# A transformer step's feed-forward input matrix: seven products of quarter sums in place of eight of quarters

## The chip, the cores and the metric

The kernel runs on one core of a Trainium2 chip. The metric is the time of one execution on the device, in microseconds (us); lower is better. A core has five engines that run side by side and wait for each other by semaphores: TensorE (PE, matmuls into the PSUM memory), VectorE (DVE), ScalarE (ACT), GpSimd (POOL) and SyncE (SP, which issues the DMAs here). Each works through its own instructions strictly in the order in which they were issued.

## The reference

One step of a one-layer hybrid encoder on 544 tokens (512 of a prompt, 32 of a sample), model width 1024: a norm, a combined input projection, three branches (differential attention, a gated linear recurrence, cross-attention), gates, an output projection; then the feed-forward block, which is what the change is about:

```
h2 = rms_norm(x, norm_ffn)
g_ff, u_ff = split(h2 @ w_ffn_in, 2)      # w_ffn_in: 1024 x 5632, so two halves of 2816
x = x + (silu(g_ff) * u_ff) @ w_ffn_out   # w_ffn_out: 2816 x 1024
y = rms_norm(x, norm_final)
```

All is float32. The kernel multiplies at that precision with three matmuls in a fast rounded format: each operand is split into a rounded part ("hi", made by ACT, line 236) and the remainder ("lo", made by DVE with `LO`, line 249), and hi x hi, hi x lo and lo x hi are added up in PSUM.

## The kernel before, in words

Activations lie transposed: 128 channels in the partitions, 8 blocks of channels (k) by 544 tokens (T) along the free side. The weights come in chunks of 1024 x 256 (1 MB each), two tiles of 128 output channels per chunk. `load_weights` fetches chunk after chunk into two raw buffers, `split_weights` splits each tile (128 x 1024) into hi (ACT) and lo (DVE); three buffers of each stand between it and PE. `gemm` runs a tile: 8 k x 2 halves of the tokens (272 columns each) x 3 = 48 matmuls into an accumulator of two PSUM banks (two accumulators, "acc"), and then spawns the tile's evacuation.

The feed-forward block has 22 chunks of w_ffn_in, 11 for the gate and 11 for the up half, in three parts (`FF_PARTS`). `ff_gate` multiplies the accumulator by the norm factor `rb` and applies Silu, `ff_up` multiplies by `rb` and by the gate and splits the result for the second matrix. The plain form does not need `rb` for its matmuls: the input (`xgh`, `xgl`) is x times the norm's gain, and `rb` comes in when the result is taken out of PSUM. `rb` itself comes from `row_norm`, spawned by `out_evac` after the last tile of the output projection (w_out). The order of stages is in for part 0, in 1, out 0, in 2, out 1, out 2. The last three tiles of the last out stage run in two halves of tokens, so that the final norm of the first half lies under the second.

The order of the instructions on each engine is made when the program is built. `Flow` is a planner in which every step is a generator; it counts an assumed cost for each instruction (about 1 ns per element for DVE, 0.9 for ACT, 0.4 per column for PE), and resumes a step when the buffers and results that it asked for are due by that count. What it issues first on an engine runs first there, whatever the real times are.

Of the kernel before, what the change touches and what calls it, by code (L numbers as in the profile page):

```python
# [9 lines left out]
F32 = mybir.dt.float32  # L10
F32R = mybir.dt.float32r
# [36 lines left out]
class Flow:  # L48
# [6 lines left out]
    def __init__(self):  # L55
        self.now = 0.0
        self.free = {"A": 0.0, "V": 0.0, "G": 0.0, "D": 0.0, "port": 0.0}
        self.rdy = {}
        self.heap = []
        self.blocked = []  # L60
        self.seq = 0
        self.ev = {}
        self.slots = {}

    @staticmethod
    def span(ap):
# [100 lines left out]

    def give(self, tag, at=None):
        self.slots[tag].append(self.now if at is None else at)

    def set(self, ev, at=None):
        self.ev[ev] = self.now if at is None else at
# [17 lines left out]
def hybrid_step(ctx: ExitStack, tc, io):  # L190
# [113 lines left out]
            fl.ready(out, t + 2200)  # L304
        return t + 2200

    def MM(out, lhsT, rhs, start, stop):
        nc.tensor.matmul(out, lhsT=lhsT, rhs=rhs, start=start, stop=stop)  # L308
# [42 lines left out]
    c_fi, c_fo = [None] * 3, [None] * 3  # L351
    for kind, i in (("in", 0), ("in", 1), ("out", 0), ("in", 2), ("out", 1), ("out", 2)):
# [10 lines left out]
    def load_weights():  # L363
        for i, (src, nk) in enumerate(chunks):
# [13 lines left out]
            for j in range(2):  # L378
                if ("raw", i, j) not in fl.ev:
                    fl.set(("raw", i, j), t)  # L380

    def split_weights():
        for i, (src, nk) in enumerate(chunks):
            if i in c_mem[4:]:
# [12 lines left out]
                fl.give("raw", t2)  # L397
                continue
            for j in range(2):
                yield from fl.get(("raw", i, j))  # L400
                yield from fl.take("wh", "wl")
                wh = slot_tile(wpool, [P, 8, P], F32R, "wh")[:, :nk]
                wl = slot_tile(wpool, [P, 8, P], F32R, "wl")[:, :nk]
                r = raws[i][:, :nk, j * P:(j + 1) * P]
                t = VC(wh, r) if fl.free["V"] + 1500 < fl.free["A"] else A(wh, r)
                wts[i, j] = (wh, wl)
# [4 lines left out]
            fl.give("raw", t2)  # L411

    def gemm(tiles, xh, xl, n=T, need=None):

# [3 lines left out]
        def products(acc, c, j, seq, first, last):  # L418
            wh, wl = wts[c, j]
            for q, (a, b, k) in enumerate(seq):  # L420
                w, x = (wl if a else wh), (xl if b else xh)
                for hf, m in halves:
                    s = slice(hf * m, (hf + 1) * m)
                    MM(acc[:, hf, :m], w[:, k, :], x[k][:, s] if isinstance(x, list) else x[:, k, s],
                       start=first and q == 0, stop=last and q == len(seq) - 1)
                yield None

        def finish(acc, c, j, evac):
            fl.give("wh")
            fl.give("wl")  # L430
            fl.spawn(evac(acc), fl.now + 60)

        if need is None:
# [1090 lines left out]
        return go  # L1524


    acts = [None] * 3

    def ff_gate(i, n):
        def go(acc):  # L1530
# [25 lines left out]
            fl.set(("f", i, n), t)  # L1556
        return go

    def ffn_in(i):
        f0, nf = FF_PARTS[i]  # L1560
        pool, a, b = (actp, "ah", "al") if i % 2 == 0 else (S["actb"], "bh", "bl")
        acts[i] = (tl(pool, [P, KD, T], F32R, a), tl(pool, [P, KD, T], F32R, b))
        for c in range(nf // 2):
            need = (lambda k: ("xg", k)) if i == 0 and c == 0 else None
            yield from gemm([(c_fi[i][c][0], j, ff_gate(i, 2 * c + j)) for j in range(2)], xgh, xgl, need=need)
            yield from gemm([(c_fi[i][c][1], j, ff_up(i, 2 * c + j)) for j in range(2)], xgh, xgl)

    def fo_evac(fp, i, n):
        def go(acc):
            t = VT(b2(x2[:, n]), acc[:, :, :HT], b2(x2[:, n]), OP.add)  # L1570
            give_acc(t)
            if i < 2:
                return
            yield t
            yield from square_sum(S["sq"][0], n)
        return go
# [42 lines left out]
    def ffn_out(fp, i):  # L1619
        f0, nf = FF_PARTS[i]  # L1620
        fh, flo = acts[i]
        split = 0 if i < 2 else LAST
# [7 lines left out]
        for t0, m_ in ((0, 256), (256, T - 256)):  # L1630
            for c, j, n in tiles[KD - split:]:
# [3 lines left out]
                for q, (a, k) in enumerate([(a, k) for a in range(2) for k in range(nf)]):  # L1635
                    if a == 1 and k == 0:
                        yield from fl.get(("wl", c, j))
                    for x in (fh, flo) if a == 0 else (fh,):
                        MM(acc, wts[c, j][a][:, k], x[:, k, t0:t0 + m_], q == 0 and x is fh,
                           q == 2 * nf - 1)  # L1640
                    yield None
                fl.spawn(last_evac(fp, n, (t0, m_), acc), fl.now + 60)
# [5 lines left out]
    def main():  # L1648
# [77 lines left out]
        xgh = tl(hpool, [P, KD, T], F32R, "hh")  # L1726
        xgl = tl(hpool, [P, KD, T], F32R, "hl")
# [3 lines left out]
        yield from ffn_in(0)  # L1731
        yield from ffn_in(1)
# [12 lines left out]
def host_arrays(inputs):  # L1745
# [71 lines left out]
```

## Time and profile before

| | |
|---|---|
| three runs, us | 1231.04, 1229.99, 1230.53; median 1230.53 |
| profiled execution, us | 1230.78, its span 1229.0 |
| busy in the span | PE 1214.2 us (99%), DVE 678.9 (55%), ACT 466.0 (38%), POOL 28.2 (2%) |
| DMA | 131.19 MB, mean 107 GB/s |
| mean granted clock of TensorE | 0.993 |

Busy time of an engine is the time in which one of its instructions ran; the span goes from the first to the last instruction. A matmul's shown duration overlaps with its neighbours', so its price is read from start to start. The granted clock is the share of TensorE's full 2.4 GHz; it has two levels, 0.5 and 1.

### The profile page before, as it was taken

The numbers are of one execution on the slowest core, as the hardware profiler recorded it, in microseconds if no ns is written. First come the engines' busy times: TensorE is split into PE (matmuls) and PEld (weight loads), VectorE is DVE, ScalarE is ACT, GpSimd is POOL, SyncE is SP. The second block draws the span as 40 slices with busy tenths as digits, with TensorE's granted clock in tenths as the row PEclk, the third lists the DMA queues.
The fourth block names the chain that finished last, engine by engine and source line by source line (L and its number), as shares of the span: only waits on it lengthen the run. The fifth ranks groups of instructions, "written<-read, shape, count | busy, mean of one in ns | idle before, by whom it ended". The sixth has DMA issues, their size and how long they took to land.

```text
span 1229.0 us, 22475 instructions
## 1 busy us (share of the span) xinstructions
PE 1214.2 (99%) x9620; PEld 1205.5 (98%) x9620; DVE 678.9 (55%) x1340; ACT 466.0 (38%) x781; POOL 28.2 (2%) x88
## 2 busy tenths in 40 slices
PE   8999999999999999999999999999999999999996
PEld 8999999999999999999999999999999999999996
DVE  6886878787257777654455244544443443344335
ACT  6635454444335665532333232332222221222122
POOL 0002000000001001000000000000000000000001
PEclk8999999999999999999999999999999999999998
DMA  7772343321222223323422413131323222222212
GB/s 261 233 272 96 133 138 116 106 87 54 103 97 94 78 73 109 122 69 121 140 95 76 176 69 104 69 104 69 103 70 103 72 101 90 82 96 77 87 52 73
DMA packets 36835, 131.19 MB, mean 107 GB/s; under 512 B 4184, under 2 KB 15832, under 8 KB 25088
## 3 DMA queue, kind: packets, MB, share of 16 engines
q1 hardware_dynamic: 36736, 129.76, 30.9%
q8 instruction: 75, 1.23, 0.4%
q14 instruction: 24, 0.20, 0.0%
HBM read 118.81 MB, written 13.68 MB: 108 GB/s over the span
## 4 chain that ended last, share of the span: by engine, by line
PE 96%; DVE 2%; DMA 1%; ACT 0%; issue 0%; SPq 0%; DVEq 0%; ACTq 0%
PE acc L308 86%; PE side L308 8%; PE side L315 2%; DMA mk_d<-mkf 1%; DMA raw<-in_w_mem_kv 0%; DVE x L258 0%; DVE wl L249 0%; DVE xT L258 0%; DVE rst L249 0%; DVE al L249 0%; ACT wh L236 0%; DVE m L249 0%; ACT m L236 0%; SPq L300 0%; DVE hl L249 0%
## 5 line engine op out<-in xcount | busy, mean ns | idle before, releaser
L308 PE MATMUL acc<-hh,wh 128*128 128x272 f32 x1856 | 387.1, 289 | 0.0
L308 PE MATMUL acc<-hl,wh 128*128 128x272 f32 x1856 | 385.8, 289 | 0.0
L236 ACT ACTIVATE wh<-raw 128x1024 fp32r<-128x1024 f32 (+1 forms) x179 | 187.4, 1048 | 351.2 <-PE acc L308 328.3
L308 PEld LDWEIGHTS acc<-hh,wh 128*128 128x128 f32 x1856 | 290.7, 189 | 0.3
L308 PEld LDWEIGHTS acc<-hl,wh 128*128 128x128 f32 x1856 | 290.0, 188 | 0.1
L249 DVE TENSOR_TENSOR wl<-raw,wh 128x1024 fp32r<-128x1024 f32 (+1 forms) x180 | 217.1, 1207 | 95.6 <-PE acc L308 73.6
L308 PE MATMUL acc<-hh,wl 128*128 128x272 f32 x1856 | 257.2, 288 | 0.0
L308 PEld LDWEIGHTS acc<-hh,wl 128*128 128x128 f32 x1856 | 241.5, 188 | 0.1
L249 DVE TENSOR_TENSOR t<-acc,rb 128x544 f32<-128x544 f32 x44 | 31.9, 725 | 150.3 <-PE acc L308 150.0
L308 PE MATMUL acc<-ah,wh 128*128 128x272 f32 (+2 forms) x480 | 101.4, 288 | 0.0
L308 PE MATMUL acc<-al,wh 128*128 128x272 f32 (+2 forms) x480 | 101.4, 289 | 0.0
L249 DVE TENSOR_TENSOR x<-acc,x 128x544 f32<-128x544 f32 (+2 forms) x35 | 23.6, 675 | 102.7 <-PE acc L308 102.7
L308 PE MATMUL acc<-bl,wh 128*128 128x272 f32 x384 | 79.7, 289 | 0.0
L308 PE MATMUL acc<-bh,wh 128*128 128x272 f32 x384 | 79.6, 288 | 0.0
L308 PEld LDWEIGHTS acc<-ah,wh 128*128 128x128 f32 x480 | 76.4, 188 | 0.0
L308 PEld LDWEIGHTS acc<-al,wh 128*128 128x128 f32 x480 | 76.2, 188 | 0.0
L308 PE MATMUL acc<-ah,wl 128*128 128x272 f32 (+2 forms) x480 | 66.0, 288 | 0.0
L308 PEld LDWEIGHTS acc<-ah,wl 128*128 128x128 f32 x480 | 62.4, 188 | 0.0
L308 PEld LDWEIGHTS acc<-bh,wh 128*128 128x128 f32 x384 | 60.1, 189 | 0.0
L308 PEld LDWEIGHTS acc<-bl,wh 128*128 128x128 f32 x384 | 60.0, 188 | 0.0
L308 PE MATMUL acc<-bh,wl 128*128 128x272 f32 x384 | 54.0, 289 | 0.0
L308 PEld LDWEIGHTS acc<-bh,wl 128*128 128x128 f32 x384 | 50.0, 188 | 0.0
(250 smaller groups left out, 1318.1 us busy)
## 6 DMA issues: line engine op xcount, KB each, us to landing
raw<-in_w_in SPq DMA_DIRECT2D x24, 1024.0 KB, 4.9
raw<-in_w_ffn_in SPq DMA_DIRECT2D x22, 1024.0 KB, 4.9
raw<-in_w_gate SPq DMA_DIRECT2D x12, 1024.0 KB, 4.9
raw<-in_w_ffn_out SPq DMA_DIRECT2D x8, 1024.0 KB, 4.9
raw<-in_w_mem_kv SPq DMA_DIRECT2D x7, 1024.0 KB, 6.1
raw<-in_w_proj_a SPq DMA_DIRECT2D x4, 1024.0 KB, 4.9
raw<-in_w_proj_b SPq DMA_DIRECT2D x4, 1024.0 KB, 4.8
raw<-in_w_proj_c SPq DMA_DIRECT2D x4, 1024.0 KB, 4.9
```

The costliest lines, as they stand in the source:

```text
L236: nc.scalar.activation(out, in_, func, scale=scale, bias=bias, accum_out=accum_out)
L249: nc.vector.tensor_tensor(out, a, b, o)
L308: nc.tensor.matmul(out, lhsT=lhsT, rhs=rhs, start=start, stop=stop)
L315: nc.tensor.transpose(out, in_, ident[:n, :n])
```

## The change

Take a chunk's 1024 x 256 weights as 2 x 2 quarters: by output tile (first or second 128 columns) and by k (even or odd blocks of channels). Take the activations as 2 x 2 quarters: by k (even, odd) and by tokens (first, second 272). Eight products of quarters make the four quarters of the result; Winograd's form of Strassen's scheme does it with seven products of sums of quarters. Of the 22 chunks, the first gate chunk and the first up chunk (`FF_PLAIN`) stay as they were; the other 20 (`FF_FAST`) use seven products, each of 4 k-blocks x 3 = 12 matmuls of 272 columns.

- **Weights.** `split_ffn` splits blocks of 128 x 512 (a quarter or a sum of quarters) in place of tiles; the three buffers are cut into six such blocks, and two more come from the space of `ah`/`al` after the plain chunks. The four sums of a chunk are made by DVE, mostly in place in the raw buffer. A22 and P4 of a chunk are split after A11 of the next (`split_late`), and the raw buffer is given back then. The host stores w_ffn_in so that each quarter is contiguous.
- **Activations.** `ff_forms` makes the normalised activations (with `rb` in them) and their sums once, in four groups (B11, B2, U1, U2), each split in hi and lo.
- **Products.** `seven` runs the products of a chunk in the order A11, (A22 and P4 of the chunk before), A12, P2, P1, P3. P2 and P3 go on adding to the accumulator of A11; between them `quarters` copies the state out: events c11 (after A11), c12 (after P2), u3 (after P3) and c22 (the sum with P1's bank).
- **Parts.** Four parts of 6, 6, 6 and 4 tiles in place of three, in the order in 0 and 1, out 0, in 2, out 1, in 3, out 2, out 3; the seven products run in three runs, of 5, 3 and 2 pairs of gate and up chunk.

```diff
-    FF_PARTS = [(0, 8), (8, 8), (16, 6)]
+    FF_PARTS = [(0, 6), (6, 6), (12, 6), (18, 4)]
+    FF_ORDER = [("in", 0), ("in", 1), ("out", 0), ("in", 2), ("out", 1), ("in", 3), ("out", 2), ("out", 3)]
+    FF_PLAIN = c_fi[0][0]
+    FF_FAST = {c for part in c_fi for pair in part for c in pair} - set(FF_PLAIN)
...
+    def split(name, src):
+        yield from fl.take("hb", "lb")
+        n = src.shape[1]
+        h_, l_ = [fl.pick(g).rearrange("p (a b) -> p a b", b=P)[:, :n] for g in ("hb", "lb")]
+        t = A(h_, src)
+        blocks[name] = (h_, l_)
+        fl.set(("bh", name), t)
+        yield t
+        fl.set(("bl", name), LO(l_, src, h_))
...
+    def split_ffn():
+        for tag, w_ in (("wh", "hb"), ("wl", "lb")):
+            for _ in range(NB[tag]):
+                yield from fl.take(tag)
+                w = slot_tile(wpool, [P, 8, P], F32R, tag).rearrange("p a b -> p (a b)")
+                add_blocks(w_, [w[:, :512], w[:, 512:]])
+        order = [c for kind, q in FF_ORDER for c in
+                 ([c for pair in c_fi[q] for c in pair] if kind == "in" else c_fo[q])]
+        late = None
+        for i in order:
+            nk = chunks[i][1]
+            yield from fl.get(("raw", i, 0))
+            if late is not None and i not in FF_FAST:
+                yield from late
+                late = None
...
+            r = raws[i].rearrange("p a b -> p (a b)")
+            q = [r[:, 512 * a:512 * (a + 1)] for a in range(4)]
+            b4 = lambda ap: ap.rearrange("p (i c) -> p i c", c=P)
+            yield from split((i, "A11"), b4(q[0]))
+            if late is not None:
+                yield from late
+            yield from split((i, "A12"), b4(q[1]))
+            yield from fl.take("xb")
+            xb = fl.pick("xb")
+            a22, p1, p2, p3 = q[3], xb, q[0], q[2]
+            VT(p1, q[2], q[3], OP.add)
+            VT(p3, q[2], q[0], OP.add)
+            VT(p2, p1, q[0], OP.add)
+            yield from split((i, "P2"), b4(p2))
+            yield from split((i, "P1"), b4(p1))
+            yield from split((i, "P3"), b4(p3))
+            late = split_late(i, b4, a22, q[1], p2, xb)
+    def split_late(i, b4, a22, a12, p2, xb):
+        yield from split((i, "A22"), b4(a22))
+        VT(a12, p2, a12, OP.add)
+        yield from split((i, "P4"), b4(a12))
+        t = fl.ev["bl", (i, "P4")]
+        fl.give("raw", t)
+        fl.drop("xb", xb, t)
...
+    def ff_forms():
+        bt, blt, ht, hlt, mt = S["bh"], S["bl"], S["xhh"], S["xhl"], S["xm"]
+        half = 4 * T
+        two = lambda ap: ap.rearrange("p (i t) -> p i t", i=4)
+        B11 = (two(bt[:, 6 * T:]), two(blt[:, 6 * T:]))
+        B2 = (two(ht[:, :half]), two(hlt[:, :half]))
+        U1 = (two(ht[:, half:]), two(hlt[:, half:]))
+        U2 = (two(mt[:, :half]), two(mt[:, half:]))
+        lo, hi = slice(0, HT), slice(HT, T)
+        for nme, grp, ev, cs in (("A11", B11, "B11", lo), ("A12", B2, "B2", lo), ("P4", B2, "B2", hi), ("P1", U1, "U1", lo),
+                                 ("P2", U1, "U1", hi), ("P3", U2, "U2", lo), ("A22", U2, "U2", hi)):
+            XF[nme] = (*grp, cs, ev)
+        yield from fl.take("ft", "ft", "ft")
+        scratch = [fl.pick("ft") for _ in range(3)] + [S["sq"][1]]
+        yield from fl.get("rb")
+        for i in range(4):
+            y0, y1, u1, u2 = scratch
+            for q, y in enumerate((y0, y1)):
+                t = VX(y, x2[:, 2 * i + q], vcol("norm_ffn", 2 * i + q), S["rb"], OP.mult, OP.mult)
+            yield t
+            A(B11[0][:, i], y0[:, lo])
+            A(B2[0][:, i], y1)
+            VT(u1[:, lo], y0[:, lo], y0[:, hi], OP.subtract)
+            VX(u1[:, hi], u1[:, lo], -1.0, y1[:, hi], OP.mult, OP.subtract)
+            VT(u2[:, lo], y1[:, hi], y0[:, hi], OP.subtract)
+            t = VX(u2[:, hi], u1[:, hi], -1.0, y1[:, lo], OP.mult, OP.subtract)
+            fl.set(("xf", "B11", i), LO(B11[1][:, i], y0[:, lo], B11[0][:, i]))
+            fl.set(("xf", "B2", i), LO(B2[1][:, i], y1, B2[0][:, i]))
+            yield t
+            for g, ev, u in ((U1, "U1", u1), (U2, "U2", u2)):
+                yield A(g[0][:, i], u)
+                t = LO(g[1][:, i], u, g[0][:, i])
+                fl.set(("xf", ev, i), t)
+        for y in scratch[:3]:
+            fl.drop("ft", y, t)
+    def seven(run):
+        def product(dst, c, form, first, last):
+            fl.set(("at", c, form))
+            yield from fl.get(("bh", (c, form)))
+            xh, xl, cs, ev = XF[form]
+            wh, wl = blocks[c, form]
+            for i in range(4):
+                yield from fl.get(("xf", ev, i))
+                MM(dst, wh[:, i], xh[:, i, cs], first and i == 0, False, True)
+                MM(dst, wh[:, i], xl[:, i, cs], False, False, True)
+                yield None
+            yield from fl.get(("bl", (c, form)))
+            for i in range(4):
+                MM(dst, wl[:, i], xh[:, i, cs], False, last and i == 3, True)
+            release((c, form))
+            fl.set(("done", c, form), fl.now + 60)
+            yield None
+        prev = None
+        for c, evac in run + [(None, None)]:
+            if c is not None:
+                yield from fl.take("acc")
+                acc = slot_tile(accp, [P, 2, 512], F32, "acc")
+                a, c_ = acc[:, 0, :HT], acc[:, 1, :HT]
+                S["b", c] = None
+                fl.spawn(evac(c, a, c_))
+                yield from product(a, c, "A11", True, False)
+            if prev is not None:
+                yield from fl.get(("u3", prev[0]))
+                yield from product(prev[1], prev[0], "A22", False, True)
+                yield from fl.get(("c22", prev[0]))
+                yield from product(prev[2], prev[0], "P4", False, True)
+            if c is None:
+                return
+            yield from product(c_, c, "A12", True, True)
+            yield from fl.get(("c11", c))
+            yield from product(a, c, "P2", False, False)
+            yield from fl.take("side")
+            b = side_tile()[:, :HT]
+            S["b", c] = b
+            yield from product(b, c, "P1", True, False)
+            yield from fl.get(("c12", c))
+            yield from product(a, c, "P3", False, False)
+            prev = c, a, b
+    def quarters(c, new, a, c_, each):
+        lo, hi = slice(0, HT), slice(HT, T)
+        yield from fl.get(("done", c, "A11"))
+        t0 = yield from new()
+        t = A(t0[:, lo], a)
+        fl.set(("c11", c), t)
+        yield from fl.get(("done", c, "A12"))
+        t = VT(t0[:, lo], c_, t0[:, lo], OP.add)
+        yield t
+        each(t0, 0, lo, t0[:, lo])
+        yield from fl.get(("done", c, "P2"))
+        t = A(t0[:, hi], a)
+        fl.set(("c12", c), t)
+        yield from fl.get(("done", c, "P1"), ("done", c, "P3"))
+        b = S["b", c]
+        t1 = yield from new()
+        t = A(t1[:, hi], a)
+        fl.set(("u3", c), t)
+        yield t
+        t = VT(t1[:, hi], b, t1[:, hi], OP.add)
+        fl.set(("c22", c), t)
+        yield t
+        each(t1, 1, hi, t1[:, hi])
+        yield from fl.get(("done", c, "A22"))
+        each(t1, 1, lo, a)
+        give_acc(fl.when(t1[:, lo]))
+        yield from fl.get(("done", c, "P4"))
+        t = VT(t0[:, hi], b, t0[:, hi], OP.add)
+        fl.give("side", t)
+        yield t
+        each(t0, 0, hi, t0[:, hi])
+        return t0, t1
...
+    def fast_gate(i, n):
...
+        def go(c, a, c_):
+            def each(g, j, cs, src):
+                A(g[:, cs], src, AF.Silu, scale=-1.0 if j else 1.0)
+            g = yield from quarters(c, new, a, c_, each)
+            S["fg", i, n] = g
+            fl.set(("fg", i, n), fl.when(g[0]))
+        return go
+    def fast_up(i, n):
...
+        def go(c, a, c_):
+            def each(u, j, cs, src):
+                if j:
+                    VX(u[:, cs], src, -1.0, S["fg", i, n][1][:, cs], OP.mult, OP.mult)
+            u = yield from quarters(c, new, a, c_, each)
+            g = S["fg", i, n]
+            t = VT(u[0], u[0], g[0], OP.mult)
+            for q in g:
+                fl.drop("ft", q, t)
+            fh, flo = acts[i]
+            for j in (1, 0):
+                yield A(fh[:, n + j], u[j])
+                t = LO(flo[:, n + j], u[j], fh[:, n + j])
+                fl.give("t1", t)
+                fl.set(("f", i, n + j), t)
+        return go
...
+        fl.spawn(ff_forms())
+        yield from ffn_in(0, 1)
         yield from ffn_out(fp, 0)
         yield from ffn_in(2)
         yield from ffn_out(fp, 1)
+        yield from ffn_in(3)
         yield from ffn_out(fp, 2)
+        yield from ffn_out(fp, 3)
...
+    w = a["w_ffn_in"]
+    a["w_ffn_in"] = w.reshape(-1, P, 4, 2, 2, P).transpose(0, 1, 4, 3, 2, 5).reshape(w.shape)
```

## Rows read from the trace of the kernel before

**Rows 1.** The page's table of engines: busy us, share of the span, instructions.
```profile
PE 1214.2 (99%) x9620; PEld 1205.5 (98%) x9620; DVE 678.9 (55%) x1340; ACT 466.0 (38%) x781; POOL 28.2 (2%) x88
```
**Rows 2.** The page's chain that ended last, shares of the span by engine.
```profile
PE 96%; DVE 2%; DMA 1%; ACT 0%; issue 0%; SPq 0%; DVEq 0%; ACTq 0%
```
**Rows 3.** Busy time by stretches: the start, the input stage, the output stage.
```profile
core 0: us, PE busy (x) PEld busy (x) DVE busy (x) ACT busy (x) POOL busy (x), PEclk, DMA share, GB/s
10.00:15.00 5.00, 5.00 (x28) 5.00 (x28) 2.65 (x6) 2.69 (x6) 0.00 (x0) 0.58 0.89 342
...
865.00:937.00 72.00, 72.00 (x576) 72.00 (x575) 30.34 (x36) 20.65 (x24) 0.00 (x0) 1.00 0.26 87
...
1140.00:1180.00 40.00, 40.00 (x321) 40.00 (x320) 12.20 (x14) 6.79 (x7) 0.00 (x0) 1.00 0.23 81
```
**Rows 4.** Timeline of PE (start us, us, what): first matmuls of two tiles following.
```profile
834.54 0.41 PE L308 MATMUL acc<-hh,wh 128*128 128x272 f32 x2
...
840.56 0.41 PE L308 MATMUL acc<-hh,wh 128*128 128x272 f32 x2
```
**Rows 5.** Timeline of PE: first matmuls of two split tiles following, 18 apart.
```profile
1200.66 0.28 PE L308 MATMUL acc<-ah,wh 128*128 128x256 f32 x1
...
1202.78 0.28 PE L308 MATMUL acc<-ah,wh 128*128 128x256 f32 x1
```
**Rows 6.** Timeline of DVE at the start of the input stage.
```profile
816.20 0.78 DVE L258 SCALAR_TENSOR_TENSOR hl<-x,vec,hh 128x544 fp32r<-128x544 f32 x1
816.89 0.72 DVE L249 TENSOR_TENSOR sqa<-sqa,t 128x544 f32<-128x544 f32 x1
...
825.11 0.72 DVE L249 TENSOR_TENSOR t<-acc,rb 128x544 f32<-128x544 f32 x1 [0.30 <-ACT rb L236]
...
834.74 0.72 DVE L249 TENSOR_TENSOR t<-acc,rb 128x544 f32<-128x544 f32 x1 [4.17 <-PE acc L308]
835.50 0.73 DVE L249 TENSOR_TENSOR t<-t,t 128x544 f32<-128x544 f32 x1
836.14 1.22 DVE L249 TENSOR_TENSOR wl<-raw,wh 128x1024 fp32r<-128x1024 f32 x1
```
**Rows 7.** Timeline of DVE where it is busy without a break.
```profile
303.40 0.42 DVE L249 TENSOR_TENSOR oS<-oS,rsy 128x256 f32<-128x256 f32 x1
303.74 1.22 DVE L249 TENSOR_TENSOR wl<-raw,wh 128x1024 fp32r<-128x1024 f32 x1
304.88 0.68 DVE L249 TENSOR_TENSOR on<-on,rsy 128x512 f32<-128x512 f32 x1
305.48 1.22 DVE L249 TENSOR_TENSOR wl<-raw,wh 128x1024 fp32r<-128x1024 f32 x1
```
**Rows 8.** Timeline of PE near the start of the kernel, after an idle time.
```profile
7.91 0.58 PE L308 MATMUL acc<-memh,wh 128*128 128x256 f32 x1 [2.56 <-ACT wh L236]
...
13.82 0.41 PE L308 MATMUL acc<-meml,wh 128*128 128x256 f32 x1
14.03 0.35 PE L308 MATMUL acc<-memh,wh 128*128 128x256 f32 x1
14.22 0.28 PE L308 MATMUL acc<-meml,wh 128*128 128x256 f32 x1
```
**Rows 9.** Timelines: DVE takes a finished tile; PE's next tile.
```profile
814.42 0.72 DVE L249 TENSOR_TENSOR x<-acc,x 128x544 f32<-128x544 f32 x1 [2.84 <-PE acc L308]
...
814.22 0.41 PE L308 MATMUL acc<-hh,wh 128*128 128x272 f32 x2
```
**Rows 10.** Timeline of ACT: one of 544, one from PSUM of 256.
```profile
826.39 0.66 ACT L236 ACTIVATE t<-t 128x544 f32<-128x544 f32 x1
...
1213.35 0.38 ACT L236 ACTIVATE t<-side 128x256 f32<-128x256 f32 x1 [0.78 <-PE side L308]
```
**Rows 11.** The page's DMA issues: count, KB each, median us to landing.
```profile
raw<-in_w_ffn_in SPq DMA_DIRECT2D x22, 1024.0 KB, 4.9
```
**Rows 12.** Timeline at the end: GpSimd's last group, the last tile's remainder matmuls.
```profile
1213.88 4.90 POOL L274 TENSOR_TENSOR x<-x,t 128x256 f32<-128x256 f32 x6 [705.79 <-ACT t L236]
...
1214.76 0.96 PE L308 MATMUL acc<-ah,wl 128*128 128x288 f32 x6
```

More of the change, by code (lines that the diff above doesn't have):

```diff
@@ L169, in give, with ring, drop, pick @@
         self.slots[tag].append(self.now if at is None else at)
+    def ring(self, tag, aps, at=None):
+        for ap in aps:
+            self.drop(tag, ap, at)
+    def drop(self, tag, ap, at=None):
+        t = self.now if at is None else at
+        self.slots.setdefault(tag, []).append(t)
+        self.seq += 1
+        heapq.heappush(self.places.setdefault(tag, []), (t, self.seq, ap))
+    def pick(self, tag):
+        return heapq.heappop(self.places[tag])[2]
     def set(self, ev, at=None):
@@ L305, in dma, with MM @@
         return t + 2200
-    def MM(out, lhsT, rhs, start, stop):
-        nc.tensor.matmul(out, lhsT=lhsT, rhs=rhs, start=start, stop=stop)
+    def MM(out, lhsT, rhs, start, stop, shared=False):
+        nc.tensor.matmul(out, lhsT=lhsT, rhs=rhs, start=start, stop=stop, skip_group_check=shared)
         n = nfree(out)
@@ L380, in load_weights, with release @@
                     fl.set(("raw", i, j), t)
+    def split(name, src):
[7 more added lines that the diff above has]
+        fl.set(("bl", name), LO(l_, src, h_))
+    def release(name):
+        for tag, ap in zip(("hb", "lb"), blocks.pop(name)):
+            fl.drop(tag, block_of(ap))
@@ new lines, in block_of, with add_blocks @@
+    def block_of(ap):
+        return places[ap.tensor.name, fl.span(ap)[0]]
+    blocks = {}
+    places = {}
+    def add_blocks(tag, aps):
+        for ap in aps:
+            places[ap.tensor.name, fl.span(ap)[0]] = ap
+        fl.ring(tag, aps)
+    def split_ffn():
[13 more added lines that the diff above has]
+                late = None
+            if i not in FF_FAST:
+                for j in range(2):
+                    if i in FF_PLAIN:
+                        r = raws[i].rearrange("p a b -> p (a b)").rearrange("p (j e i c) -> p j e i c", j=2, e=2, i=4)
+                        for e in range(2):
+                            yield from split((i, j, e), r[:, j, e])
+                        ks = [((i, j, k % 2), k // 2) for k in range(nk)]
+                    else:
+                        for e in range(0, nk, 4):
+                            yield from split((i, j, e), raws[i][:, e:min(e + 4, nk), j * P:(j + 1) * P])
+                        ks = [((i, j, k // 4 * 4), k % 4) for k in range(nk)]
+                    wts[i, j] = tuple([blocks[b][a][:, q] for b, q in ks] for a in range(2))
+                    names = sorted({b for b, _ in ks})
+                    frees[i, j] = names
+                    fl.set(("wh", i, j), max(fl.ev["bh", b] for b in names))
+                    fl.set(("wl", i, j), max(fl.ev["bl", b] for b in names))
+                fl.give("raw", max(fl.ev["bl", b] for b in names))
+                continue
+            r = raws[i].rearrange("p a b -> p (a b)")
[15 more added lines that the diff above has]
+            late = split_late(i, b4, a22, q[1], p2, xb)
@@ L405, in split_weights @@
                 t = VC(wh, r) if fl.free["V"] + 1500 < fl.free["A"] else A(wh, r)
-                wts[i, j] = (wh, wl)
+                wts[i, j] = tuple([w[:, k] for k in range(nk)] for w in (wh, wl))
                 yield t
@@ L411, in split_weights, with free_weights @@
             fl.give("raw", t2)
+    def free_weights(c, j):
+        if (c, j) in frees:
+            for b in frees[c, j]:
+                release(b)
+        else:
+            fl.give("wh")
+            fl.give("wl")
     def gemm(tiles, xh, xl, n=T, need=None):
@@ L428, in finish @@
         def finish(acc, c, j, evac):
-            fl.give("wh")
-            fl.give("wl")
+            free_weights(c, j)
             fl.spawn(evac(acc), fl.now + 60)
@@ new lines, in fast_gate, with new @@
+    def fast_gate(i, n):
+        def new():
+            yield from fl.take("ft")
+            return fl.pick("ft")
+        def go(c, a, c_):
[6 more added lines that the diff above has]
+    def fast_up(i, n):
+        def new():
+            yield from fl.take("t1")
+            return t1_tile()
+        def go(c, a, c_):
[14 more added lines that the diff above has]
+        return go
@@ L1557, in ff_up, with ffn_plain, ffn_in @@
         return go
[L1559 to L1566, printed above, removed]
+    def ffn_plain():
+        need = lambda k: ("xg", k)
+        g, u = FF_PLAIN
+        yield from gemm([(g, j, ff_gate(0, j)) for j in range(2)], xgh, xgl, need=need)
+        yield from gemm([(u, j, ff_up(0, j)) for j in range(2)], xgh, xgl)
+    def ffn_in(*parts):
+        run = []
+        for i in parts:
+            x = ("bh", "bl") if i % 2 == 0 else ("ah", "al")
+            for q in range(len(c_fi[i])):
+                if (i, q) != (0, 0):
+                    run += [(c_fi[i][q][0], fast_gate(i, 2 * q)), (c_fi[i][q][1], fast_up(i, 2 * q))]
+            acts[i] = [S[n][:, :6 * T].rearrange("p (k t) -> p k t", k=6) for n in x]
+        if 0 in parts:
+            yield from ffn_plain()
+            for tag, nme in (("hb", "ah"), ("lb", "al")):
+                add_blocks(tag, [S[nme][:, 6 * T:6 * T + 512], S[nme][:, 6 * T + 512:6 * T + 1024]])
+        yield from seven(run)
     def fo_evac(fp, i, n):
```

37 lines of the change are left out of this document (26 added, 11 removed).

## The prediction

> **What bounds the kernel now.** First the table of engines on the page: TensorE (PE) is busy for 99% of the span, VectorE (DVE) for 55%, ScalarE (ACT) for 38% [rows 1]. Then the chain that ended last: 96% of it is PE [rows 2]. The table by stretches shows the same for the part that the change touches: in the feed-forward input stage PE is busy without a gap at granted clock 1.00, DVE for 42% of the time, in the output stage for 31% [rows 3]. So matmuls that are taken out shorten the time one for one, as long as the other engines keep up; and a gap that is put into PE lengthens it one for one.
>
> **Matmuls removed.** One output tile of 48 matmuls of 272 columns lasts from 834.54 to 840.56: 0.1254 us each [rows 4]. A chunk of the weight (two tiles) has 96; as seven products of 12 it has 84. 20 of the 22 chunks are changed: 20 x 12 x 0.1254 = 30.1 us less. A product then takes 12 x 0.1254 = 1.505 us (called a slot below). That all 12 go to one PSUM bank costs nothing: the split tiles at the end do so already, 18 matmuls of 256 columns from 1200.66 to 1202.78 without a gap [rows 5].
>
> **DVE's new load.** Start to start, independent DVE instructions take 0.60 us for 512 elements, 0.64 for 544 (0.69 with a per-partition factor) and 0.34 for 256 [rows 6, 7]; 272 elements are not shown, I take 0.37, by the slope from 256 to 544. One that needs the result just before it takes 0.11 longer (0.76 for 544) [rows 6]. A pair of chunks (gate, up) costs DVE: 14 remainders and 8 weight sums of 512 (22 x 0.60 = 13.2), 8 of 272 (3.0), 3 of 544 (1.9): 18.1 us in a pair of 14 slots, 21.1 us. It fits, at 86%, but the order matters: DVE and ACT work strictly in the order of issue.
> The Trainium skill (VectorE: DVE Perf Modes, "The DRAIN you can't avoid") says that the next DVE instruction does not start until the pipe is empty, so that each would cost its full duration (0.68 for 512 in [rows 7]). The trace does not bear that out where nothing is waited for: there 0.60 passes from start to start. By the rule the pair would cost some 20.6 us; what full durations would do here is rival 3.
>
> **The start of the fast products.** They need four new forms of the activations, each for i = 0 to 3. ff_forms waits for rb, at 825.1 [rows 6], and makes i after i; the first product needs the form B11 of all four. A pass of ff_forms is two normalisations (1.38), four differences of 272 (0.37 x 3 + 0.48), one remainder of 272 and three of 544 (2.30): 5.27 us of DVE. Up to the last B11 that is 3 x 5.27 + 3.34 = 19.1 us. PE has only the two plain chunks to do meanwhile, till 840.6 [rows 4]. And ff_forms does not have DVE alone: whatever is ready is queued as it comes, and the weight splits are ready as soon as a block is free. Before the last B11 I count: 2 remainders of the plain up chunk, then 8 blocks' worth (five products of the first fast chunk, A11 of the second, A22 and P4 of the first), 10 x 0.60; 4 weight sums, 2.4; 4 evacuations of plain tiles, 2 products of gate and up and 2 remainders, 8 x 0.645. That is 13.6 us. DVE is at it from 825.1 to 825.1 + 32.7 = 857.8. PE can do six matmuls of A11 (i = 0 to 2, 0.75 us) ahead: it idles for 857.8 - 840.6 - 0.75 + 0.2 for the two hand-overs = 16.7 us. Bounds: 3.1 if ff_forms went first throughout (19.1 in place of 32.7), 20.8 with DVE's full durations.
> After that PE runs slower. In the trace it idles for 2.56 us near the start and then issues 256-column matmuls every 0.21 us, at granted clock 1.2 GHz, from 7.91 to 14.03, and from 14.22 on every 0.12 [rows 3, 5, 8]: 6.3 us at about 0.55 of the pace, 2.8 us lost. I add 2.8; the bounds are 0 and 3.2 (half of 6.3).
>
> **Waits inside a pair.** Product P3 accumulates on what P2 left, so it waits until ACT has copied that out ("c12"). P1, one slot, stands between. The copy is issued after the addition of A12 (DVE) and the Silu that needs it, and behind both stand others. Take the end of P4 of the up chunk before as 0, in a gate chunk: P3 could start at 3 slots, 4.52. An engine starts 0.20 after PE's next matmul has started [rows 9]. ACT splits A12 of the next chunk from 0.20 to 0.84 (0.64 for 512: a little under the 0.66 for 544 [rows 10]); DVE makes the remainder (0.9 to 1.5), three weight sums (to 3.3), the product of up and gate (to 3.95), and only then the addition. ACT waits for the third sum, splits P2 (3.43), then the finished activation (4.07, it waited for the product), P1 (4.63), Silu (5.16), copy (5.47 to 5.86; 0.38 for 256 columns from PSUM [rows 10], 0.39 taken). With some 0.15 to PE (an estimate, a little under the 0.20 the other way) P3 starts at 6.0: 1.5 us late. This happens in each gate chunk that follows an up chunk of its run: 4 + 2 + 1 = 7, 10.5 us. In an up chunk there is no Silu and no product of gate and up in front: the copy ends at 4.35, 0.0 late. In the first gate chunk of the second and third run I find 0.3, together 0.6. Bounds per wait: 0, if the queued work is issued after the copy, and 2.1 with full durations. The other waits (c11, c22, u3) have one to three slots and need 1.25 (0.2, a split 0.53, the copy 0.39, 0.15): nothing.
> At the end of a run no product stands between P3 and A22: 1.25 us each, three runs, 3.8. Bounds 0.7 (no split in front of the copy) and 2.
>
> **What costs nothing.** A weight load takes 4.9 us [rows 11]. Its buffer is given back later than before (after P4, one chunk on), about 1.6 us after the end of A22, and is wanted again five slots after that end, 7.5 us: 1 us to spare, and seven more products lie ready behind it. SP's queue holds only these loads there. If the loads were late, ACT's split would stand in front of the copies, up to 1 us a chunk. At the change from w_out to the plain chunks all three buffers must be free first, but the first is, by 6 us, before PE gets there. In four output parts in place of three there are as many matmuls, and 8 more evacuations on a DVE that is 69% idle [rows 3].
> **The tail.** The last part has 4 k-tiles in place of 6, so the second half of the last three tiles is 3 x 6 matmuls shorter, 2.4 us, in which the first half's normalisation was hidden; the 4.9 us of GpSimd then run beside the last chain [rows 12]. DVE's small instructions slowed down beside it. I take 1.0, between 0 and 2.
>
> **Sum:** -30.1 + 16.7 + 2.8 + 10.5 + 0.6 + 3.8 + 1.0 = +5.3 us. The profiled execution took 1230.78 (span 1229.0), 0.25 above the median of the runs; so 1235.8 for the median, 1236.
>
> **Rivals.**
> 1. The copies are not held up (the order of issue comes out kinder than I traced it, or the Silu is not in front). Then 11.1 us go: 1225. For it: the margin hangs on the order of five ACT instructions; against it: the chain P2 sum, split, copy is strict in the code.
> 2. The start is short: ff_forms gets DVE nearly alone, PE idles for 3 us and keeps its clock; the waits in the pairs stay. 16.7 + 2.8 - 3.1 = 16.4 less: 1219.4, faster. It decides from the point where the weight splits stay behind the forms in DVE's queue. Against it: the splits are issued when a block is free, and six are while the forms are under way.
> 3. DVE works at full durations: 4.1 more at the start (36.8 us of DVE in place of 32.7), 2.1 in place of 1.5 in seven waits, 8.3 us more: 1244. For it: much of the new work waits for ACT or for a result just made; against it: the rows with 0.60.
> That eight products become seven and PE simply keeps up (1230.5 - 30.1 = 1200) I give no chance of its own: the 19.1 us of forms alone exclude it.
>
> **How the numbers follow.** Forecast 0.52 (1236, its own range 1229 to 1243), rival 1 0.16, rival 2 0.11, rival 3 0.21. Faster by over 0.2% (below 1228.1; 2.5 us is about what this kernel's runs can tell from no change): rival 2, most of rival 1 (0.12) and 0.02 of the forecast, 0.25. Same: 0.04 of rival 1, 0.10 of the forecast, 0.14. Slower: 0.61. The range 1219 to 1247 takes in rivals 1 and 3 and the upper half of rival 2.
>
> **What would show it.** In the trace after: PE idle from about 841 to 858 with waits for bh or hh on DVE or ACT, and a granted clock of 0.5 for some 6 us behind it; DVE busy without a break from 825 to 858; waits of about 1.5 us of PE on ACT's copy in every second chunk, and 1.2 at the end of three runs; 240 matmuls fewer. It is wrong if PE idles for under 10 us at the start, if the waits in the pairs are under 0.5 us, or if DVE, not the copies, holds PE all through the stage.

## The result, and the profile after

The changed kernel takes 1291.27 us (1286.34 to 1293.01 in four runs) where the kernel before takes 1230.78 beside it: a ratio of 1.0486, with 95% between 1.0456 and 1.0516. It is slower, by 60.5 us; 5.3 were forecast, and the upper end of the range was 1247. The profiled execution has a span of 1288.6 us at a mean granted clock of 0.970.

The page's table of engines and its chain, of the kernel after (they answer to [rows 1, 2]):
```profile
PE 1214.2 (94%) x9380; PEld 1198.0 (93%) x9380; DVE 801.4 (62%) x1634; ACT 540.2 (42%) x1013; POOL 28.2 (2%) x88
...
PE 87%; DVE 9%; ACT 2%; DMA 1%; issue 1%; SPq 0%; DVEq 0%; ACTq 0%
```
There are 240 matmuls fewer, as planned, and yet PE is busy for the same 1214.2 us. It is idle for 74 us of the span, and DVE, whose share of the chain was 2%, now has 9%. The saved 30 us are not in the busy time either: the matmuls that are left became slower.

The table by stretches, of the kernel after. The first row answers to the input stage in [rows 3]; the others go with the readings below (columns: PE, its weight loads, DVE, ACT and POOL, each busy us; then granted clock, DMA share, GB/s).
```profile
core 0: us, PE busy (x) PEld busy (x) DVE busy (x) ACT busy (x) POOL busy (x), PEclk, DMA share, GB/s
865.00:937.00 72.00, 60.64 (x438) 59.54 (x437) 47.48 (x81) 33.05 (x68) 0.00 (x0) 0.92 0.22 74
841.00:860.00 19.00, 5.34 (x28) 4.32 (x27) 18.44 (x34) 8.34 (x16) 0.00 (x0) 0.64 0.17 56
888.00:891.30 3.30, 0.28 (x4) 0.07 (x2) 3.23 (x7) 0.30 (x1) 0.00 (x0) 0.93 0.80 258
891.30:894.20 2.90, 2.90 (x13) 2.90 (x14) 1.81 (x3) 1.44 (x4) 0.00 (x0) 0.50 0.18 73
894.20:897.00 2.80, 2.80 (x24) 2.80 (x24) 1.38 (x2) 1.61 (x4) 0.00 (x0) 1.00 0.00 0
```
In the same 72 us PE now does 438 matmuls, not 576, and has gaps and a clock of 0.92. One gap is the stretch from 888.0 to 891.3, in which DVE is busy and PE is not. In the 2.9 us behind it PE is never idle and does 13 matmuls, where it does 24 in the next 2.8: the clock was 0.50.

What PE waits for, over the whole span of the kernel after (us in total, times, longest):
```profile
PE acc L325 <- DVE fq L265: 24.0, 10, 3.0
PE acc L325 <- DVE t L265: 14.0, 10, 1.8
...
PE acc L325 <- ACT fq L252: 5.2, 4, 1.3
...
PE acc L325 <- ACT t L252: 1.5, 3, 0.5
```
The first two rows are new, 20 waits, one for each chunk that takes seven products. The other two belong to the run starts and run ends; the copies that the prediction feared are hardly there.

PE around one of the longest of these waits, in a gate chunk of the kernel after:
```profile
887.36 0.67 PE L325 MATMUL acc<-hh,al 128*128 128x272 f32 x4
887.86 0.29 PE L325 MATMUL acc<-hh,wh 128*128 128x272 f32 x1
887.99 0.29 PE L325 MATMUL acc<-hl,wh 128*128 128x272 f32 x1
891.29 0.59 PE L325 MATMUL acc<-hh,wh 128*128 128x272 f32 x1 [3.02 <-DVE fq L265]
```
And DVE in the same time:
```profile
887.51 0.72 DVE L265 TENSOR_TENSOR t<-t,fq 128x544 f32<-128x544 f32 x1
888.15 0.68 DVE L265 TENSOR_TENSOR al<-raw,ah 128x512 fp32r<-128x512 f32 x1
888.75 0.68 DVE L265 TENSOR_TENSOR fb<-raw 128x512 f32<-128x512 f32 x1
889.47 0.69 DVE L265 TENSOR_TENSOR raw<-raw 128x512 f32<-128x512 f32 x1
890.19 0.69 DVE L265 TENSOR_TENSOR raw<-fb,raw 128x512 f32<-128x512 f32 x1
890.80 0.43 DVE L265 TENSOR_TENSOR fq<-acc,fq 128x272 f32<-128x272 f32 x1
```
A12 is done at 888.0 (first row of PE), two matmuls of P2 have gone, and the third starts only when DVE's last row, the addition that reads A12's result from PSUM, has run. DVE takes a remainder and three weight sums first. But P2 does not write where A12 lies: P2 adds to bank 0 of the accumulator, A12 is in bank 1. Both banks are one tile (`acc`, two halves), and the program orders by tiles. In the instruction order it is P2's third matmul that carries a wait on DVE; the addition is recorded after the first two. The theory (A) from here: this wait, which nothing in the arithmetic asks for, costs the time, directly and by the clock. The rivals: (B) DVE cannot keep up with four sums a chunk; (C) the blocks of weights are too few; (D) the start, with what follows from it.

### The profile page after: what moved, and what is told of

Read it like the earlier page. It is cut to its first block, busy times and chain, and to the rows that moved or that the text cites. A ratio compares the mean times of both kernels' runs of the same rounds, so it can differ in the third digit from the quotient of the medians.

```text
span 1288.6 us, 22679 instructions
## 1 busy us (share of the span) xinstructions
PE 1214.2 (94%) x9380; PEld 1198.0 (93%) x9380; DVE 801.4 (62%) x1634; ACT 540.2 (42%) x1013; POOL 28.2 (2%) x88
## 4 chain that ended last, share of the span: by engine, by line
PE 87%; DVE 9%; ACT 2%; DMA 1%; issue 1%; SPq 0%; DVEq 0%; ACTq 0%
PE acc L325 73%; PE side L325 13%; DVE raw L265 2%; DVE wl L265 2%; PE side L332 2%; DVE t L265 1%; DMA raw<-in_w_mem_kv 1%; ACT wh L252 1%; DVE fb L265 1%; DVE al L265 1%; DVE fq L265 1%; DVE x L274 0%; DVE xT L274 0%; DVE rst L265 0%; DVE m L265 0%
## 5 line engine op out<-in xcount | busy, mean ns | idle before, releaser
L252 ACT ACTIVATE wh<-raw 128x1024 fp32r<-128x1024 f32 (+2 forms) x251 | 201.1, 803 | 310.1 <-PE acc L325 210.6
L265 DVE TENSOR_TENSOR wl<-raw,wh 128x512 fp32r<-128x512 f32 (+1 forms) x252 | 226.4, 905 | 128.1 <-PE acc L325 78.6
L325 PE MATMUL acc<-hh,wh 128*128 128x272 f32 x1268 | 277.0, 293 | 29.2 <-DVE fq L265 18.0
L325 PE MATMUL acc<-hl,wh 128*128 128x272 f32 x1268 | 273.5, 291 | 0.0
L325 PEld LDWEIGHTS acc<-hh,wh 128*128 128x128 f32 x1268 | 204.9, 190 | 33.1 <-DVE fq L265 19.8
L325 PEld LDWEIGHTS acc<-hl,wh 128*128 128x128 f32 x1268 | 204.7, 190 | 0.1
L325 PE MATMUL acc<-hh,wl 128*128 128x272 f32 x1268 | 184.2, 292 | 0.0
L325 PEld LDWEIGHTS acc<-hh,wl 128*128 128x128 f32 x1268 | 169.9, 191 | 0.1
L325 PE MATMUL acc<-bh,wh 128*128 128x272 f32 x464 | 100.3, 289 | 12.1 <-ACT bh L252 12.1
L252 ACT ACTIVATE ah<-raw 128x512 fp32r<-128x512 f32 (+1 forms) x44 | 26.5, 602 | 60.6 <-DVE raw L265 26.9
```

What stands on the lines that cost most here:

```text
L252: nc.scalar.activation(out, in_, func, scale=scale, bias=bias, accum_out=accum_out)
L265: nc.vector.tensor_tensor(out, a, b, o)
```

## The experiments

**1. A product in a bank of its own.** A12 goes to a tile of its own, so that P2 shares nothing with the addition; the sums stay where they were.
```
             yield from fl.take("side")
+            c_ = side_tile()[:, :HT]
+            S["c_", c] = c_
             yield from product(c_, c, "A12", True, True)
...
-        t = VT(t0[:, lo], c_, t0[:, lo], OP.add)
+        t = VT(t0[:, lo], S["c_", c], t0[:, lo], OP.add)
+        fl.give("side", t)
```
(`a` is then half of `acc` alone.)

> One edit to the changed kernel: the product A12 goes into a PSUM tile of its own (one of the four side banks) in place of the second bank of the accumulator's tile. Theory A (the accumulator's two banks are one tile to the program, so P2's matmuls wait until DVE has read A12 out of the other bank, and that addition stands behind three weight sums; each wait of about 3 us lets the clock fall as well): the 20 waits of PE on DVE (38 us) are gone; in their place about 1.7 us on ACT's copy before P3 in up to ten gate chunks; granted clock 1.00 outside the start; 1240 to 1252 us. Theory B (DVE is too full, whatever PE waits for first): the waits move to other places with the same sum, 1280 to 1292.

Measured: 1250.57 us, 1.0162 of before [1.0144, 1.0179]: 40.7 us less than after, with the same DVE work. All 20 waits on DVE are gone, and another row has come:
```profile
PE acc L325 <- ACT fq L252: 17.9, 11, 1.9
```
ACT and PE of this kernel at one of them (timelines):
```profile
889.33 0.63 ACT L252 ACTIVATE ah<-raw 128x512 fp32r<-128x512 f32 x1 [3.71 <-DVE raw L265]
889.86 0.64 ACT L252 ACTIVATE bh<-t 128x544 fp32r<-128x544 f32 x1
890.41 0.41 ACT L252 ACTIVATE fq<-fq 128x272 f32<-128x272 f32 x1
890.73 0.37 ACT L252 ACTIVATE fq<-acc 128x272 f32<-128x272 f32 x1
```
```profile
891.15 1.02 PE L325 MATMUL acc<-m,wh 128*128 128x272 f32 x6 [1.82 <-ACT fq L252]
```
This is the wait that was forecast: ACT stands 3.71 us for the third sum, then come the split of P2, another split, the Silu, the copy, and P3 starts 1.82 us late. In the changed kernel these waits are missing; that P2's own wait had let ACT catch up there is the likely reason, not one that a run singles out. So A holds, and B falls for the largest part. One thing that was expected did not come: the granted clock still fell behind three of the new waits (last section).

**2. The sums behind the addition.** The tile stays shared; the three sums wait until the addition of the previous chunk's A12 is in DVE's queue, and the splits of P2 and P4 are queued when their sums are due.
```
+            if behind is not None:
+                yield from fl.get(("added", behind))
+            behind = i
...
-            VT(p2, p1, q[0], OP.add)
+            yield VT(p2, p1, q[0], OP.add)
...
-        VT(a12, p2, a12, OP.add)
+        yield VT(a12, p2, a12, OP.add)
```
(In `quarters`, `fl.set(("added", c))` after the addition.)

> One edit to the changed kernel: the order on DVE. The three weight sums of a chunk are issued only when the addition of A12 of the chunk before has been issued, and the splits of P2 and P4 only when their sums are due; the shared accumulator tile stays. Theory A: P2 still waits for the addition, but this now comes first: about 0.65 us a chunk in place of 1.9, 13 us in all, no wait over 1 us, granted clock 1.00 outside the start: 1238 to 1255. Theory B (DVE too full): DVE has as much to do, the waits stay at 35 us or more: 1280 to 1295.

Measured: 1245.57 us, 1.0119 [1.0101, 1.0136]. The waits:
```profile
PE acc L325 <- DVE fq L265: 8.2, 10, 1.7
...
PE acc L325 <- DVE t L265: 5.2, 9, 0.9
```
On DVE the addition now comes ahead of the sums (in one up chunk it starts at 896.48, the first sum at 900.11); the waits fall from 38.0 to 13.4 us, and no clock falls behind them. No wait over 1 us was expected; three are 1.7, 1.0 and 1.0. What is left of them is the shared tile: P2 still waits for the addition itself.

**3. Both.**

> Both edits, own bank and sums behind the addition. Theory A: no wait before P2, and the copy before P3 no longer stands behind a split that waits for a sum: under 8 us of waits inside the pairs; what is left against the kernel before is the start (about 14 us idle and 3 of clock) and three run ends of 1.3, against 30 saved: 1222 to 1236. Theory B: 1275 or more.

Measured: 1224.91 us, 0.9954 [0.9939, 0.9969], half a per cent under the kernel before. Inside the pairs no wait on the addition or on a copy is left, only two on splits of weights, 0.8 and 0.3 us; the start (7.6 and 5.5 us) and the ends of the runs (three times 0.5) remain:
```profile
PE acc L325 <- ACT bh L252: 7.6, 2, 4.6
PE acc L325 <- DVE bl L265: 5.5, 2, 4.0
```
DVE does the same instructions here, 797 us of them; as a bound (B) it is out.

**4. A second plain pair at the start.** PE has two more plain chunks to do while the new forms are made; inside the pairs nothing is changed.
```
-    FF_PLAIN = c_fi[0][0]
+    NPLAIN = 2
+    FF_PLAIN = [c for pair in c_fi[0][:NPLAIN] for c in pair]
```
(`ffn_plain` loops over both pairs, `ffn_in` leaves both out.)

> One edit to the changed kernel: the first two pairs of chunks stay plain in place of one, so that PE has 24 us more of its own work while DVE makes the forms of the activations; everything else as in the changed kernel. If the start costs what the trace shows (13.6 us idle between 843.4 and 858.8 and some 3 us of low clock): -17, 3 us more for two plain chunks, and one pair's waits and clock less (about 7): 1268 to 1275. If the idle time at the start is hidden elsewhere (DVE's backlog only moves): 1285 to 1295.

Measured: 1251.73 us, 1.0175 [1.0150, 1.0200]; the expectation missed by 16 us, on the good side. The start came out as it said. The stretch in which PE was idle before, and then the waits, of this kernel:
```profile
845.00:862.00 17.00, 17.00 (x138) 17.00 (x137) 16.86 (x32) 8.79 (x15) 0.00 (x0) 1.00 0.18 63
```
```profile
PE acc L325 <- DVE fq L265: 14.1, 9, 3.0
PE acc L325 <- DVE t L265: 8.5, 9, 1.8
```
But the waits inside the pairs shrank as well, by 15.4 us, all in the first run; 3.5 of them stood in the pair that is plain now. DVE's timeline there has the other order, by itself: the addition first, the sums after.
```profile
893.27 0.43 DVE L265 TENSOR_TENSOR fq<-acc,fq 128x272 f32<-128x272 f32 x1
...
895.46 0.69 DVE L265 TENSOR_TENSOR fb<-raw 128x512 f32<-128x512 f32 x1
```
The order of issue depends on which block comes free when, and another start shifts that. The sum from rows: 13.65 of start and 15.4 of waits less; behind them half-speed time worth 12.6 us less (19.5 in the kernel after, at the start and behind the waits, 6.9 here; worked out as under the reasons below); 24 matmuls more, 3.0; ACT's waits (fq and t) 1.7 more; together 37.0 less. Measured are 39.5 less; 1.5 of the rest is a stretch at half clock in the first plain chunk that this run does not have (see the sum under the reasons).

**5. All three.** Bank, sums and second plain pair.

> Own bank, sums behind the addition, and two plain pairs at the start. Theory A, with the start's price as read from the trace (13 us idle and 2 to 3 us of low clock, for 3 us of two more plain chunks): 12 to 14 us under own bank and sums behind alone: 1210 to 1214. If the forms' idle time only moves on: 1220 or more.

Measured: 1210.52 us (1210.26 to 1215.69 in four runs), 0.9849 [0.9828, 0.9869]. This is the fastest version, 20 us under the kernel before. The stretch of the former gap, and the page's table of engines:
```profile
845.00:870.00 25.00, 25.00 (x202) 25.00 (x201) 23.39 (x43) 12.48 (x22) 0.00 (x0) 1.00 0.13 44
```
```profile
PE 1189.2 (98%) x9404; PEld 1178.4 (98%) x9404; DVE 787.5 (65%) x1617; ACT 531.4 (44%) x999; POOL 28.2 (2%) x88
```
With 216 matmuls fewer (27.1 us) the busy time is 25.0 us lower: here nearly all of the saving arrives. From the third kernel to this one 14.4 us go, where 12 to 14 were expected: that is D, the start, at its own price.

**6. Six blocks of weights instead of eight.** If blocks were short (C), fewer must cost more.
```
-            for tag, nme in (("hb", "ah"), ("lb", "al")):
-                add_blocks(tag, [S[nme][:, 6 * T:6 * T + 512], S[nme][:, 6 * T + 512:6 * T + 1024]])
```

> One edit to the changed kernel: six weight blocks in place of eight (the two from the space of the old activations are not added), so that each split is issued two products later. Nothing of the work changes. Theory A (what counts is whether the sums stand in front of the addition on DVE; with six blocks they are issued behind it): waits before P2 of 0.5 to 1.0 us in place of 1.8 and 3.0, no fall of the clock after them: 1236 to 1256. If a longer lead of the weights is what PE needs: 1291 or slower.

Measured: 1247.32 us, 1.0135 [1.0118, 1.0152], 44 us faster than with eight. The waits:
```profile
PE acc L325 <- DVE fq L265: 9.1, 10, 1.0
...
PE acc L325 <- DVE t L265: 5.3, 10, 0.5
```
Fewer blocks hold the next chunk's splits and sums back, so they come after the addition. C falls; the effect has the opposite sign. What hurt was work done early, on an engine that takes its instructions in order.

**7. Own bank, and the splits queued when their sums are due** (the first edit and the two `yield VT(...)` of the second, without the sums waiting).

> Own bank, and only the second half of the reordering: the splits of P2 and P4 are issued when their sums are due, the sums themselves stay where they were, in front of the addition. It tells apart the two things that can hold the copy before P3 with an own bank (17.9 us in eleven waits): if it is ACT's split that waits for a sum with the copy behind it, those waits shrink under 6 us: 1230 to 1240; if it is the Silu behind the addition, which stands behind the sums, they stay at 12 us or more: 1243 to 1252.

Measured: 1233.19 us, 1.0027 [1.0016, 1.0038].
```profile
PE acc L325 <- ACT fq L252: 6.3, 5, 1.3
```
Against the first experiment 17.4 us go, and ACT's copies cause 6.3 us of waits, not 17.9, a little over the "under 6" that was expected. By its time the run speaks for the split, but its trace does not separate the two causes. In the second and third run the three sums came behind the addition on DVE by themselves, as in experiment 3, and the waits there are gone with both causes. In the first run the sums still stand in front of the addition, and P2's split still stands in front of the Silu and the copy. The addition on DVE, and ACT behind it, in the same gate chunk as above:
```profile
890.79 0.43 DVE L265 TENSOR_TENSOR fq<-side,fq 128x272 f32<-128x272 f32 x1
```
```profile
890.98 0.63 ACT L252 ACTIVATE ah<-raw 128x512 fp32r<-128x512 f32 x1 [2.08 <-DVE raw L265]
891.52 0.41 ACT L252 ACTIVATE fq<-fq 128x272 f32<-128x272 f32 x1
```
P3 is 1.27 us late there, four times, in place of 1.82. The Silu (last row) starts 0.3 after the addition that it needs is done (891.2), so P2's split can hold it by 0.3 at most; the rest of the 1.27 comes from the addition's place behind the sums. In the first experiment's rows the Silu starts at 890.41, and the addition was done at 889.56:
```profile
889.13 0.43 DVE L265 TENSOR_TENSOR fq<-side,fq 128x272 f32<-128x272 f32 x1
```
So the two splits in front of it account for 0.85 of the 1.82 at most. Both the addition and the splits hold the copy, and the weight sums stand in front of both.

**8. Twelve useless matmuls before each P2** (240 more, to a scratch bank, so the output is the same). The instruction order of DVE and ACT is that of the changed kernel.
```
+            ws = side_tile()[:, :HT]
+            for q in range(12):
+                nc.tensor.matmul(ws, lhsT=blocks[c, "P2"][0][:, q % 4],
+                                 rhs=XF["A12"][0][:, q % 4, lo_], start=True, stop=True, ...)
```

> The changed kernel with 12 useless matmuls (one slot, 1.5 us of work, into a side bank that nobody reads) in front of each P2, where PE waits for DVE; 240 in all, as many as the change took away. DVE and ACT have the same instructions in the same order as in the changed kernel. If the clock's fall after the seven waits of 3.0 us is what costs the rest (PE is busy for 1214.2 us before and after, with 240 matmuls fewer): the idle part of these waits shrinks to 1.5 us, the granted clock stays at 1.00 after them, some 25 us of slow matmuls go, and the filler adds 1.0 to 1.5 us in the five chunks with waits under 1.5: 1266 to 1276, faster with 240 matmuls more. If the matmuls are slow for another reason, or the waits alone cost the time: 1290 or more.

Measured: 1278.28 us, 1.0394 [1.0377, 1.0412], 13.0 us *faster* with 240 matmuls more. Waits, the same gate chunk, and the stretch behind its wait:
```profile
PE acc L325 <- DVE fq L265: 10.6, 7, 1.5
PE acc L325 <- DVE t L265: 5.3, 10, 0.5
```
```profile
889.66 0.39 PE L325 MATMUL acc<-hh,wh 128*128 128x272 f32 x1 [1.51 <-DVE fq L265]
```
```profile
889.70:893.70 4.00, 4.00 (x32) 4.00 (x33) 3.16 (x5) 2.73 (x6) 0.00 (x0) 1.00 0.10 41
```
The time is 2.3 us above the range expected if the clock is the cause, and 11.7 under the other. Behind the wait the clock is 1.00 and 32 matmuls go in 4.0 us. The filler is 240 x 0.1254 = 30.1 us; the two rows are 22.1 us shorter, ACT's 1.2 (5.2 to 4.0); that makes 6.8 more. So some 20 us came from elsewhere, and the only other thing seen to change is the clock: between 888 and 1200 us it stays at 1.00 here. DVE and ACT have the same instructions in the same order in both traces.

## Why the prediction was wrong

**The step that failed** is in "Waits inside a pair": the first wait was taken to be P3's, and "The other waits (c11, c22, u3) have one to three slots and need 1.25 [...]: nothing". P2 was given no wait but c11. It has one on the addition of A12. The prediction even had the time of that addition: it starts "to 3.95" after the end of P4. From a DVE addition's start to PE's next matmul the trace after shows 0.49 (890.80 to 891.29), so P2's third matmul goes at 4.44; it could have gone at 1.76, a slot and two matmuls. That is 2.7 late by the forecast's own times; 3.02 of idle time was measured. Reading the two banks as two things, from the code, cost the forecast; `acc` is one tile.

**The clock inside the stage** was not in the sum. The forecast priced a low clock behind the start alone. In the trace after, it fell behind each of the seven waits of 3.0 us and behind two of the seven of 1.78 (which end at 934.20 and 964.84), for 2.9 to 6.2 us of PE's busy time each. Counted over stretches of 2 us, PE is busy for 39.7 us at 0.50 between 888 and 1200; matmuls are then 0.225 apart instead of 0.125, so 44% of it is lost, 17.6 us. The eighth experiment removes this part, and with it the 1.5 us of the next paragraph, and gives some 20 us: the same size.

**The sum as it came out**, against the forecast's terms: -30.1 for the matmuls (as forecast); idle start 13.65 (forecast 16.7); low clock at the start 1.9 (forecast 2.8); P2's waits 38.0 (forecast none); low clock inside the runs 17.6 (none); the plain chunks end at 842.78 instead of 840.56, 2.2 (none); copies at the run starts 5.2 and at the run ends 1.5 (forecast, with the seven in the gate chunks, 14.9). The 2.2 has its own cause, and the forecast had no term for it: early in the first plain chunk PE waits 0.93 us for the squares of the norm, a wait that the kernel before does not have, and the next stretch runs at half clock:
```profile
817.82 1.27 PE L325 MATMUL side<-ones_d,sqa 128*128 128x1 f32 x10 [0.93 <-DVE sqa L265]
```
```profile
819.20:822.50 3.30, 3.30 (x16) 3.30 (x16) 2.41 (x13) 1.27 (x2) 0.00 (x0) 0.50 0.95 318
```
In the 3.4 us at half clock 15 matmuls start, which take 1.5 us more than at the usual pace. All the terms together are 50.0 of the 59.6 by which the span grew. Each wait also costs what lies beside its idle time: from 887.99 to 891.29 are 3.30 us, of which 3.02 are idle and 0.125 is the usual pace, so 0.155 more is spent, and that 27 times, 4.2. The tail's waits are 1.2 us longer (forecast 1.0). About 4 us stay open.

**What held.** The start, shown here by PE and DVE of the kernel after:
```profile
851.68 0.60 PE L325 MATMUL acc<-bh,wh 128*128 128x272 f32 x1 [8.23 <-ACT bh L252]
...
856.65 0.59 PE L325 MATMUL acc<-bh,wh 128*128 128x272 f32 x1 [3.90 <-ACT bh L252]
...
858.76 0.60 PE L325 MATMUL acc<-bl,wh 128*128 128x272 f32 x1 [1.52 <-DVE bl L265]
```
```profile
826.53 1.48 DVE L274 SCALAR_TENSOR_TENSOR fq<-x,vec,rb 128x544 f32<-128x544 f32 x2
...
858.28 0.43 DVE L265 TENSOR_TENSOR bl<-fq,bh 128x272 fp32r<-128x272 f32 x1
```
The last B11 is done at 858.7 where 857.8 was forecast, and the idle time comes in three pieces. It is 3.0 us shorter: it starts 2.1 later, because the plain chunks end later, it ends 0.8 later, and between its pieces PE works for 1.7 on what is ready.

**The copies** were right in mechanism, did not show in the changed kernel, and were seen in the first experiment: seven gate chunks at 1.82 where 1.5 was worked out. The first gate chunks of the second and third run have 1.80 and 1.88, where 0.3 each was found. At the ends of the runs 0.49 was seen, not 1.25. The forecast's chain had both causes, the addition behind the sums and the splits in front of the Silu; by the rows of experiments 1 and 7 both have their share.

**The rivals.** Rival 2 (a short start) did not happen. Rival 3 (DVE at full durations) did not either: the rows above start 0.60 after a remainder of 0.68, and 0.72 after a sum whose result or buffer the next one needs. The forecast took 0.60 for each of 22 instructions of 512, and the dependent sums cost 0.1 more each. The Trainium skill (VectorE: DVE Perf Modes, "The DRAIN you can't avoid") has the next instruction wait for an empty pipe; the prediction drew on that sentence alone, but the same section adds that an instruction which is not held starts earlier, and 0.60 after a remainder of 0.68 agrees with that. Rival 1 (copies not held up) is what experiment 3 made true, together with the end of P2's wait, and it gave 1224.91 where rival 1 said 1225. That this is so close is partly luck: at the start 13.1 us of waits were seen where rival 1 had 16.7, at the ends of the runs 1.5 where it had 3.8, and the wait of 0.93 in the first plain chunk and the two on splits of weights were not in it. Of the signs named beforehand, "if DVE, not the copies, holds PE all through the stage" is the one that came.

## What to carry to other kernels

In this program, what two engines share as one tile is one dependency, however far apart the halves that they use are: for each wait in a forecast, list every reader of the whole tile that the next writer touches, and look where those readers stand in their engine's queue. Work that is ready early can do harm in front of work that another engine waits for; an edit that saves PE time and gives DVE more has to say where the new instructions stand. And price a wait on PE twice, once for itself and once for the matmuls behind it: here that was 38.0 and 17.6 us. Which of the shorter waits the clock will fall behind can't be told from their length by these runs, so the second price is a range.

## What the runs showed that was not expected

- 240 useless matmuls made the kernel 13.0 us faster (experiment 8).
- The granted clock fell to 0.50 behind all seven waits of 3.0 us, behind two of seven of 1.78 us, and, in experiment 1, behind three of nine of 1.8 us; behind the waits inside the pairs in experiments 2 (up to 1.7), 6 (1.0), 7 (1.3) and 8 (1.51) it stayed at 1.00. In experiment 1, behind a wait of 1.82 us that ends at 938.14 (after another of 1.82 that ends at 914.56 the same column is 1.00):
```profile
938.10:941.20 3.10, 3.06 (x14) 3.06 (x15) 1.62 (x3) 1.68 (x4) 0.00 (x0) 0.53 0.00 0
```
Why equal waits of 1.8 us differ in this was not settled.
- In the first plain chunk the clock fell behind a wait of only 0.93 us (the two rows under the sum). The changed kernel and all eight experiments have this wait; in three of these nine kernels (the changed one, experiments 6 and 7) half clock follows it, in the other six it does not.
- The start of the fast products changes the order of issue of a whole run after it (experiment 4), and so did two blocks fewer (experiment 6): one was worth 15 us of waits, the other 24.
